# mLSTM decode state update: one fused VectorE operation per sample in place of two GpSimd operations per four samples

## The chip, the cores and the metric

The kernel runs on one core of a Trainium2 chip. The metric is the device time of one execution in microseconds (us), the median over repeated runs. A profile of a single execution stands beside it. Its engines are called PE (TensorE), ACT (ScalarE), DVE (VectorE), POOL (GpSimd) and SP (SyncE, which here only issues DMAs). Each engine works through its own instructions strictly in order, and an instruction that waits holds up everything behind it on that engine.

## What is computed

One inference step of a two-layer decoder for 256 prompt tokens and 8 single-token samples, which share the weights (264 columns in all). Layer 0 mixes tokens with a convolution, layer 1 with an mLSTM; each has a convolutional feed-forward block and an embedding gate behind it. The change concerns the mLSTM state of the 8 samples, where each has a matrix memory of 128 x 256 for each of 8 heads:

```python
def step(carry, inp):                       # for a sample: one token, so one step
    c, n, m = carry
    ...
    num = (s @ v) + (q @ c) * w_inter       # the OLD c is read for the output
    ...
    g_state = jnp.exp(inter[..., -1] - m_new)
    g_tok = jnp.exp(bh[..., -1:] - bh + lih - m_new[..., None])
    c_new = g_state[..., None, None] * c + jnp.einsum('bhs,bshk,bshv->bhkv', g_tok, kc, vc)
```

For a sample the last line is: new state = a number of the head and sample times the old state, plus an outer product of k and v (v already weighted).

## The kernel before, in words

All big products go through `wblock`: a weight block of 4 x 128 rows by 512 columns is loaded by one DMA (`raw`, three buffers), ACT makes its rounded upper part (`whi`, line 234), DVE the rest (`wlo`, line 235), and PE multiplies three times for each 128 x 128 piece (lines 250, 252, 253, and 259 for a first piece). Five buffers of two such row groups let ACT and DVE run ahead of PE. The issuing order on each engine is chosen by the framework's list scheduler, which simulates the time; `high_priority` moves an instruction ahead in it, `after` fixes an order.

In layer 1, `mlstm` works on pairs of heads. `project(pr)` computes q, k, v of a pair; `heads(pr)` runs the steps of four generators in turn: `prompt` of two heads and `sample` of two heads. PE meanwhile goes on with the next products (`opened` for the gate, the next `project`). `norm` normalises the outputs of a pair: its two matmuls (`hm`, line 825, and `hq`, line 833) are put between the matmuls of a later block (`normed`), each behind a given one, and they need sums from DVE.

The change is in `Head.sample`. Per head there are two groups of four samples (`b4` = 0, 1). `Ct` (state) and `kb` (rows q and k) are pieces of the big tile `X`, which is parked in DRAM meanwhile; they show in the profile as `X`. The two heads of a pair use the same two `Ct` places, so the load of the second head's group waits for the store of the first head's group. For each group:

- SP issues the load of `Ct` (line 795) and of `kb` (796).
- DVE multiplies `Ct` with q (two operations of 128 x 512, in the profile `spare<-X`) and sums over k (`tensor_reduce`, line 801): these become the output of the samples, via four tiny 128 x 16 operations per head (`spare<-qc`, `spare<-spare,sv`, or `H<-...` for the last pair).
- ACT replaces `kb` by the outer product, eight operations of 128 x 128 (line 805).
- POOL multiplies the four states by their numbers (`X<-X,spare`) and adds `kb` (`X<-X`), each 128 x 1024.
- SP issues the store (line 808).

There are 8 heads x 2 groups = 16 groups. The helper `tt` records its operations at line 138, `stt` (scalar_tensor_tensor, DVE only) at line 141. Besides, POOL has at the end of `mlstm` four small operations for the feed-forward's past rows (`sf`, `fo`).

Of the kernel before, what the change touches and what calls it, by code (L numbers as in the profile page):

```python
# [15 lines left out]
ALU = mybir.AluOpType  # L16
AX = mybir.AxisListType

P = 128
# [89 lines left out]
def _body(ctx, tc, nc, I, O):  # L109
    PSUM = bass.MemoryType.PSUM  # L110
    v, s, g, pe, dma = nc.vector, nc.scalar, nc.gpsimd, nc.tensor, nc.sync
# [19 lines left out]
    def misc(name):  # L131
        return psM.tile([P, 512], F32, name=name, tag="mi")
# [4 lines left out]
    def tt(o, a, b, op, e=v):  # L137
        return e.tensor_tensor(o, a, b, op)  # L138

    def stt(o, a, sc, b, op0, op1):  # L140
        return v.scalar_tensor_tensor(o, a, sc, b, op0, op1)  # L141

    def after(ins, first):

        tc.add_manual_dep(ins.ins, first.ins.name, mybir.DependencyInfo(
            mybir.DependencyClass.NoSync, mybir.DependencyReason.DATA), reason="order")
# [473 lines left out]
    def mlstm(xin):  # L620
# [82 lines left out]
        class Head:  # L703
# [65 lines left out]
            def sample(self):  # L769
                h, vh, H, den, bwi, bwf = self.h, self.v, self.H, self.den, self.bwi, self.bwf  # L770
                qs, ks = self.q[:, SEQ:], self.k[:, SEQ:]
                qq = smp.tile([P, 2, NB], F32, name="qq", bufs=2)
                tt(qq[:, 0], qs, ks, ALU.mult)
                tt(qq[:, 1], qs, sn[:, h], ALU.mult)
                nf = smp.tile([P, NB], F32, name="nf", bufs=2)
                tt(nf, sn[:, h], bwf, ALU.mult)
                tt(NS[:, h], ks, bwi, ALU.mult)
                tt(NS[:, h], NS[:, h], nf, ALU.add)
                vw = smp.tile([P, 2, NB], F32, name="vw", bufs=2)
                tt(vw, vh[:, :, SEQ:], bwi.unsqueeze(1).to_broadcast([P, 2, NB]), ALU.mult)  # L780
                psq = misc("sq")
                pe.matmul(psq[:, 0:2 * NB], ones, qq.rearrange("p a b -> p (a b)"), start=True, stop=True)
                ss = smp.tile([P, 2, NB], F32, name="ss", bufs=2)
                tt(ss, psq[:, 0:2 * NB].rearrange("p (a b) -> p a b", a=2),
                   self.bc[:, 648:664].rearrange("p (a b) -> p a b", a=2), ALU.mult)
                tt(den[:, SEQ:], ss[:, 0], ss[:, 1], ALU.add)
                stt(den[:, SEQ:], den[:, SEQ:], -1.0, den[:, SEQ:], ALU.mult, ALU.max)
                yield
                yield
                yield  # L790
                qc = smp.tile([P, NB, 2], F32, name="qc", bufs=2)
                for b4 in range(2):
                    Ct, kb = (XF[:, o + b4 * 1024:o + b4 * 1024 + 1024].rearrange("p (b x k) -> p b x k", b=4, x=2)
                              for o in (0, 2048))
                    dma.dma_start(Ct, I["cT"][h, :, 4 * b4:4 * b4 + 4])
                    dma.dma_start(kb, rows[h, 4 * b4:4 * b4 + 4].partition_broadcast(P))
                    for b2 in (0, 2):
                        qp = s1[:, 512 + 4 * T:1024 + 4 * T].rearrange("p (b x k) -> p b x k", b=2, x=2)
                        ins = tt(qp, Ct[:, b2:b2 + 2], kb[:, b2:b2 + 2, 0:1, :].to_broadcast([P, 2, 2, P]), ALU.mult)
                        after(ins, self.pt)  # L800
                        v.tensor_reduce(qc[:, 4 * b4 + b2:4 * b4 + b2 + 2], qp, AX.X, ALU.add)
                    for bi in range(4):
                        e = 4 * b4 + bi
                        for x in range(2):
                            act(kb[:, bi, x], kb[:, bi, 1], AF.Copy, scale=vw[:, x, e:e + 1])
                    tt(Ct, Ct, bwf[:, 4 * b4:4 * b4 + 4].unsqueeze(2).unsqueeze(3).to_broadcast([P, 4, 2, P]), ALU.mult, e=g)
                    tt(Ct, Ct, kb, ALU.add, e=g)
                    dma.dma_start(O["cT"][h, :, 4 * b4:4 * b4 + 4], Ct)
                    yield
                hs = H[:, :, SEQ:]  # L810
                tt(hs, qc.rearrange("p b x -> p x b"), bwf.unsqueeze(1).to_broadcast([P, 2, NB]), ALU.mult)
                sv = smp.tile([P, 2, NB], F32, name="sv", bufs=2)
                tt(sv, vh[:, :, SEQ:], ss[:, 0].unsqueeze(1).to_broadcast([P, 2, NB]), ALU.mult)
                tt(hs, hs, sv, ALU.add)
# [289 lines left out]
```

## Time and profile before

| what | us |
|---|---|
| median of 3 runs (2585.0 to 2591.87) | 2591.32 |
| the profiled execution, its own time | 2594.45 |
| its span | 2592.6 |
| PE busy | 2524.0 (97%) |
| DVE busy | 1680.9 (65%) |
| ACT busy | 1286.0 (50%) |
| POOL busy | 395.2 (15%) |

The shares are means over stages with different limits. The mLSTM stage with the sample updates lies at about 1300 to 1640 us of the span; the first of the 32 POOL operations starts at 1307.1, the last at 1614.1.

A view in order of time gives for each instruction the start and the duration in us, engine, line, operation, what is written and read, and in square brackets the idle time before it on its engine with the last releaser. Grouped views give busy time in us and the mean duration in ns.

### The profile page before, as it was taken

What the parts mean: (1) busy time and instruction counts of PE and PEld (TensorE: products, weight loads), DVE (VectorE), ACT (ScalarE), POOL (GpSimd) and SP (SyncE); (2) the same over time, 40 slices, a digit from 0 to 9 for tenths busy, and PEclk for the clock granted to TensorE, in tenths of its full rate; (3) what the DMA queues carried; (4) which work ended last, traced back from release to release, by engine and by line L of the source; (5) the groups of instructions that cost most, each with busy time, mean ns of one, the idle gap of its engine ahead of it and who ended that gap; (6) DMA issues with size and microseconds to landing.
All of it is one profiled execution on the core that took longest, in us unless ns stands there. A gap on an engine that the chain in (4) does not pass through costs nothing.

```text
span 2592.6 us, 47730 instructions
## 1 busy us (share of the span) xinstructions
PE 2524.0 (97%) x20130; PEld 2499.7 (96%) x20130; DVE 1680.9 (65%) x2318; ACT 1286.0 (50%) x1801; POOL 395.2 (15%) x352
## 2 busy tenths in 40 slices
PE   8898999999999999999989998999999999999999
PEld 8897999999999999999989998999999999999999
DVE  6999686555445555488678778685555445555595
ACT  5666555444334444356456666374444334444363
POOL 7898120000000000020031123020000000000020
PEclk9999999999999999999999999999999999999999
DMA  7546445555555556545666776645555555556554
GB/s 251 172 132 203 164 149 194 177 187 182 182 180 179 179 179 207 180 167 195 208 225 217 238 242 214 220 148 196 188 181 179 179 179 179 180 180 204 178 175 138
DMA packets 266697, 486.57 MB, mean 188 GB/s; under 512 B 12362, under 2 KB 68426, under 8 KB 265938
## 3 DMA queue, kind: packets, MB, share of 16 engines
q1 hardware_dynamic: 266482, 483.52, 56.9%
q8 instruction: 157, 2.57, 0.4%
q14 instruction: 58, 0.48, 0.1%
HBM read 465.77 MB, written 19.68 MB: 187 GB/s over the span
## 4 chain that ended last, share of the span: by engine, by line
PE 83%; DVE 6%; DMA 3%; POOL 3%; issue 2%; ACT 2%; SPq 0%; POOLq 0%; DVEq 0%; ACTq 0%
PE acc L253 27%; PE acc L250 27%; PE acc L252 23%; PE acc L259 3%; DVE wlo L235 1%; POOL cscr L138 1%; DVE Y L141 1%; DMA X<-in_cT 1%; DMA out_cT<-X 1%; DVE spare L138 1%; DVE Y L138 1%; POOL wlo L235 1%; PE acc L452 1%; ACT whi L234 1%; POOL u L504 0%
## 5 line engine op out<-in xcount | busy, mean ns | idle before, releaser
L235 DVE TENSOR_TENSOR wlo<-raw,whi 128x1024 fp32r<-128x1024 f32 (+1 forms) x770 | 977.3, 1274 | 815.0 <-ACT whi L234 767.7
L234 ACT CAST whi<-raw 128x1024 fp32r<-128x1024 f32 x812 | 846.0, 1045 | 1019.9 <-PE acc L252 972.6
L253 PE MATMUL acc<-XH,wlo 128*128 128x264 f32 x4264 | 1192.0, 286 | 14.4 <-POOL wlo L235 7.9
L250 PE MATMUL acc<-XH,whi 128*128 128x264 f32 x4264 | 1193.7, 286 | 5.9 <-ACT cscr L546 4.9
L252 PE MATMUL acc<-XL,whi 128*128 128x264 f32 x3696 | 1049.7, 285 | 0.0
L253 PEld LDWEIGHTS acc<-XH,wlo 128*128 128x128 f32 x4264 | 803.7, 189 | 17.4 <-POOL wlo L235 9.6
L250 PEld LDWEIGHTS acc<-XH,whi 128*128 128x128 f32 x4264 | 801.7, 189 | 8.3 <-ACT cscr L546 5.3
L252 PEld LDWEIGHTS acc<-XL,whi 128*128 128x128 f32 x3696 | 701.4, 190 | 0.1
L235 POOL TENSOR_TENSOR wlo<-raw,whi 128x1024 fp32r<-128x1024 f32 (+1 forms) x42 | 97.4, 2324 | 1670.3 <-DVE X L138 1506.1
L253 PE MATMUL acc<-ha,wlo 128*128 128x264 f32 x1024 | 290.2, 285 | 0.0
L250 PE MATMUL acc<-ha,whi 128*128 128x264 f32 x1024 | 288.6, 285 | 0.0
L252 PE MATMUL acc<-ha,whi 128*128 128x264 f32 x960 | 272.0, 284 | 0.0
L250 PE MATMUL acc<-xo,whi 128*128 128x264 f32 x768 | 225.4, 295 | 8.0 <-ACT so L894 6.0
L253 PE MATMUL acc<-xo,wlo 128*128 128x264 f32 x768 | 223.8, 293 | 0.0
L252 PE MATMUL acc<-xo,whi 128*128 128x264 f32 x720 | 211.3, 294 | 0.0
L253 PEld LDWEIGHTS acc<-ha,wlo 128*128 128x128 f32 x1024 | 193.2, 189 | 0.0
L250 PEld LDWEIGHTS acc<-ha,whi 128*128 128x128 f32 x1024 | 192.0, 189 | 0.1
L252 PEld LDWEIGHTS acc<-ha,whi 128*128 128x128 f32 x960 | 181.4, 189 | 0.1
L250 PEld LDWEIGHTS acc<-xo,whi 128*128 128x128 f32 x768 | 148.9, 194 | 9.5 <-ACT so L894 6.4
L253 PEld LDWEIGHTS acc<-xo,wlo 128*128 128x128 f32 x768 | 149.1, 194 | 0.8
L252 PEld LDWEIGHTS acc<-xo,whi 128*128 128x128 f32 x720 | 139.6, 194 | 0.7
L138 POOL TENSOR_TENSOR cscr<-cscr 128x254 f32<-128x254 f32 (+10 forms) x140 | 124.7, 918 | 11.5 <-ACT cscr L564 10.3
(284 smaller groups left out, 2580.0 us busy)
## 6 DMA issues: line engine op xcount, KB each, us to landing
raw<-in_ff_w_gate SPq DMA_DIRECT2D x88, 1024.0 KB, 5.1
raw<-in_ff_w_up SPq DMA_DIRECT2D x88, 1024.0 KB, 5.1
raw<-in_ff_w_down SPq DMA_DIRECT2D x88, 1024.0 KB, 5.0
raw<-in_pl_w_gate SPq DMA_DIRECT2D x32, 1024.0 KB, 5.0
raw<-in_ml_w_in SPq DMA_DIRECT2D x32, 1024.0 KB, 6.2
raw<-in_cv_w_in SPq DMA_DIRECT2D x48, 512.0 KB, 5.0
raw<-in_cv_w_out SPq DMA_DIRECT2D x16, 1024.0 KB, 5.0
raw<-in_ml_w_in SPq DMA_DIRECT2D x32, 512.0 KB, 5.3
```

Of the source, the lines that this page charges most:

```text
L138: return e.tensor_tensor(o, a, b, op)
L141: return v.scalar_tensor_tensor(o, a, sc, b, op0, op1)
L234: whi = s.copy(hi[:, :, :width], r)
L235: wlo = e.tensor_tensor(lo[:, :, :width], r, f32(hi[:, :, :width]), ALU.subtract)
L250: pe.matmul(acc[j], wh, xh, start=kc == 0, stop=False)
L252: pe.matmul(acc[j], wh, xl, start=False, stop=False)
L253: wlast[0] = pe.matmul(acc[j], wl, xh, start=False, stop=not lag and kc == nk - 1)
L259: pe.matmul(acc[j], whs[j], xl, start=False, stop=lag > 0 and k0_ == nk - 1)
L452: po(pe.matmul(acc, w[:, k, j * P:(j + 1) * P], pt[:, k], start=k == 0, stop=k == 1))
```

## The change

For each group the two POOL operations are replaced by four `scalar_tensor_tensor` operations on DVE, one per sample: Ct = Ct x number + kb, over 128 x 256. The number is read per partition from `bwf`.

```diff
                     for bi in range(4):
                         e = 4 * b4 + bi
                         for x in range(2):
                             act(kb[:, bi, x], kb[:, bi, 1], AF.Copy, scale=vw[:, x, e:e + 1])
-                    tt(Ct, Ct, bwf[:, 4 * b4:4 * b4 + 4].unsqueeze(2).unsqueeze(3).to_broadcast([P, 4, 2, P]), ALU.mult, e=g)
-                    tt(Ct, Ct, kb, ALU.add, e=g)
+                    for bi in range(4):
+                        e = 4 * b4 + bi
+                        stt(Ct[:, bi], Ct[:, bi], bwf[:, e:e + 1], kb[:, bi], ALU.mult, ALU.add)
                     dma.dma_start(O["cT"][h, :, 4 * b4:4 * b4 + 4], Ct)
                     yield
```

## Rows read from the trace of the kernel before

**Rows 1.** Per stretch: length, PE, PEld, DVE, ACT, POOL busy, clock, DMA share, GB/s

```profile
0.00:1300.00 1300.00, 1263.89 (x9995) 1247.89 (x9995) 857.69 (x1236) 655.63 (x898) 274.83 (x278) 0.99 0.57 184
1300.00:1640.00 340.00, 316.09 (x2447) 311.27 (x2448) 267.61 (x383) 204.90 (x414) 81.04 (x36) 0.96 0.68 230
1640.00:2592.00 952.00, 943.98 (x7691) 940.56 (x7689) 555.63 (x699) 425.48 (x489) 39.36 (x38) 1.00 0.55 178
```

**Rows 2.** PE in order of time, 1300 to 1640 us: its idle times over 1 us

```profile
1301.49 0.39 PE L250 MATMUL acc<-xo,whi 128*128 128x264 f32 x1 [1.97 <-ACT vv L876]
...
1338.53 0.46 PE L250 MATMUL acc<-xo,whi 128*128 128x264 f32 x1 [4.42 <-ACT so L894]
1361.31 0.71 PE L833 MATMUL hq<-hq,onesD 128*128 128x264 f32 x2 [2.02 <-DVE hq L138]
1426.09 0.39 PE L250 MATMUL acc<-xo,whi 128*128 128x264 f32 x1 [1.60 <-ACT so L894]
1451.56 1.25 PE L833 MATMUL hq<-hq,onesD 128*128 128x264 f32 x2 [4.17 <-DVE hq L138]
1516.90 1.25 PE L825 MATMUL hm<-hm,onesD 128*128 128x264 f32 x2 [2.64 <-DVE hm L138]
1595.41 1.25 PE L825 MATMUL hm<-hm,onesD 128*128 128x264 f32 x2 [4.80 <-DVE hm L138]
1617.77 0.49 PE L833 MATMUL hq<-hq,onesD 128*128 128x264 f32 x1 [1.80 <-DVE hq L138]
```

**Rows 3.** POOL, groups by form, 1300 to 1640 us: busy us, mean ns | idle

```profile
L138 POOL TENSOR_TENSOR X<-X 128x1024 f32<-128x1024 f32 x16 | 44.0, 2753 | 9.4 <-POOL X L138 4.4 <-ACT X L805 2.3 <-issue 1.5
L138 POOL TENSOR_TENSOR X<-X,spare 128x1024 f32<-128x1024 f32 x16 | 33.1, 2070 | 289.3 <-DVE spare L138 133.0 <-ACT vt L740 72.3 <-ACT X L805 69.6
```

**Rows 4.** DVE, groups by form, 1300 to 1640 us

```profile
L235 DVE TENSOR_TENSOR wlo<-raw,whi 128x1024 fp32r<-128x1024 f32 x90 | 126.4, 1405 | 37.3 <-ACT whi L234 34.1 <-PE hm L825 1.8 <-PE acc L252 1.1
L138 DVE TENSOR_TENSOR spare<-X 128x512 f32<-128x512 f32 x32 | 27.2, 850 | 14.7 <-DMA X<-in_cT 14.3
L801 DVE TENSOR_REDUCE qc<-spare 128x4 f32<-128x512 f32 x32 | 21.8, 681 | 0.6
...
L138 DVE TENSOR_TENSOR qw<-qk,spare 128x128 f32<-128x128 f32 x8 | 8.9, 1106 | 0.0
L138 DVE TENSOR_TENSOR spare<-qc,spare 128x16 f32<-128x16 f32 x6 | 8.6, 1432 | 0.1
...
L141 DVE SCALAR_TENSOR_TENSOR spare<-spare,par,so 128x264 f32<-128x264 f32 x12 | 5.3, 489 | 2.6 <-ACT so L894 2.5
...
L141 DVE SCALAR_TENSOR_TENSOR Pd<-qw,cn,spare 128x128 f32<-128x128 f32 x8 | 2.8, 346 | 0.7 <-ACT cn L746 0.6
...
L138 DVE TENSOR_TENSOR vw<-vv,spare 128x16 f32<-128x16 f32 x8 | 1.4, 171 | 0.0
```

**Rows 5.** DVE, groups by form, 1750 to 2592 us

```profile
L235 DVE TENSOR_TENSOR wlo<-raw,whi 128x1024 fp32r<-128x1024 f32 x278 | 341.0, 1231 | 349.8 <-ACT whi L234 329.0 <-PE acc L252 20.7
```

**Rows 6.** DVE in order of time, ahead of the idle time at 1361.31

```profile
1356.25 2.42 DVE L235 TENSOR_TENSOR wlo<-raw,whi 128x1024 fp32r<-128x1024 f32 x1
1358.59 2.33 DVE L138 TENSOR_TENSOR spare<-qc,spare 128x16 f32<-128x16 f32 x1
```

**Rows 7.** A stretch of 10 us, columns as in the first group

```profile
1360.00:1370.00 10.00, 8.69 (x57) 8.62 (x58) 8.91 (x20) 6.51 (x12) 0.88 (x1) 0.83 0.93 327
```

**Rows 8.** The DMA queue's waits, 1300 to 1640 us: total us, times, longest

```profile
SPq L795 <- DMA out_cT<-X: 27.9, 10, 6.3
SPq L808 <- POOL X L138: 23.9, 6, 6.6
```

**Rows 9.** DVE and ACT in order of time, one group: last reduce, last of eight scales

```profile
1398.51 0.69 DVE L801 TENSOR_REDUCE qc<-spare 128x4 f32<-128x512 f32 x1
1400.45 0.71 ACT L805 ACTIVATE X<-X,vw 128x128 f32<-128x128 f32 x2
```

**Rows 10.** POOL in order of time: the first operation of the feed-forward's past rows

```profile
1588.72 1.49 POOL L939 COPY fo<-sf 128x352 f32<-128x352 f32 x1
```

## The prediction

> **What bounds the kernel now.** I read the table of stretches first. PE is busy for nearly all of the first and last stretch, but in the mLSTM stage (1300 to 1640 us) only 316.1 of 340 us, and its granted clock is 0.96 there against 1.00 behind it [rows 1]. So PE sets the time, and this stage can give back at most what PE loses in it: 340 - 316.1 = 23.9 us idle, and by the clock about 0.04 x 340 = 13.6 us. Nothing outside the stage is touched; the stretches before and after count as they are.
>
> PE in order of time then shows that the idle time is a few stalls: 1.97, 4.42, 2.02, 1.60, 4.17, 2.64, 4.80 and 1.80 us, together 23.4 [rows 2]. The first comes before any of the POOL operations can hold anything and stays. Of the other seven (21.5 us), five wait for `hm` or `hq`, sums that DVE delivers late, and two for `so`, which ACT delivers late behind things that wait for DVE. So in this stage the engine ahead of PE is DVE: 267.6 of 340 us busy [rows 1], in order, and late at the ends of the head pairs. The question is whether the change takes time from DVE or gives it.
>
> **What goes.** POOL loses 16 + 16 operations, 33.1 + 44.0 = 77.1 us [rows 3]. Nobody waits for POOL as such except the stores. But DVE pays while POOL runs: the weight split `wlo`, the same form, takes 1405 ns on the mean here [rows 4] and 1231 ns in the later stages [rows 5]; a 128 x 16 product takes 1432 ns where another of that size takes 171; the 128 x 128 product `qw` takes 1106 ns where the fused operation of that size takes 346; the 128 x 512 products take 850 ns, the reduces of the same size 681 [rows 4]. A tiny operation at 2.33 us [rows 6], about as long as a POOL operation (2.07 and 2.75 us on the mean) [rows 3], says that DVE is held until POOL is done. The held time by those four pairs of rows: 90 x 0.174 = 15.7, 6 x 1.261 = 7.6, 8 x 0.760 = 6.1, 32 x 0.169 = 5.4: 34.8 us, a lower bound since smaller forms are left out. That is 2.2 us for each of the 16 groups. All of it goes with POOL's operations.
>
> The Trainium skill ("SBUF — State Buffer", "Who interferes with whom") says that a VectorE instruction with two SBUF inputs and a GpSimd instruction that reads SBUF exclude each other for a whole instruction, and that a reduce never contends. The trace agrees as to the reduces, 32 at a mean of 681 ns [rows 4]. By that rule the new operations, which have two SBUF inputs, can themselves be held by what POOL keeps; that is the fourth rival below.
>
> **What comes.** 64 fused operations of 128 x 256 on DVE. The trace has none of this very shape; the nearest with all inputs in SBUF and a per-partition number are 489 ns at 264 columns and 346 ns at 128 [rows 4]. The end at 346 would make 22.1 us, the end at 489 31.3 us. I take 0.40 us, an estimate: 256 lies near 264, and successive DVE operations overlap by some 0.08 us (2.42 us after 1356.25 is 1358.67, and the next starts at 1358.59 [rows 6]), so 489 ns cost the queue about 0.40. That is 25.6 us, 1.6 for a group. DVE's balance is -34.8 + 25.6 = -9 us for the stage, -0.6 per group at least.
>
> **Where it lies.** Mean values say too little, since only the groups just ahead of a stall matter. Ahead of the stall at 1361.31 the held time is 2.42 - 1.23 = 1.2 for `wlo` and 2.33 - 0.17 = 2.2 for the tiny product, 3.4 us [rows 4 to 6]; four fused operations add 1.6: 1.8 us net of a stall of 2.02. I take 0.6 to 1.8 us per group. Three of the seven stalls come behind one group (1361, 1451, 1617): 3 x 0.6 to 3 x 1.8, so 1.8 to 5.4. The other four (1338, 1426, 1516, 1595) come at the end of a pair's dense part, behind two groups: 4 x 1.2 to 2 x 3.6 + 1.6 + 2.64 (two are no longer than that), so 4.8 to 11.4. Sum: 6.6 to 16.8 us. I take 13, in the upper half, since in the one stall worked out the upper value holds, and since the held time is a lower bound.
>
> **The clock.** After a stall the granted clock is lower for a while, 0.83 in the ten us with the stall of 2.02 [rows 7], where the level falls from 2.4 to 1.2 GHz for part of the time. It goes with the stalls: 13 of 23.9 us of idle time are 54%, and 54% of 13.6 is 7 us (3 to 10 for the ends).
>
> **The queues.** SP waits 23.9 us for POOL before stores, and 27.9 us for stores before it issues the loads of the next `Ct` [rows 8]; DVE in turn waits 14.3 us for those loads [rows 4]. A group's POOL part is 2.07 + 2.75 = 4.8 us; four fused operations are 1.6, so the store goes some 3 us sooner, and the next group's load and sums with it. I count this at nothing: where it helps, it eats into the same stalls. The weight loads queue behind these waits on SP; no stall of PE names them [rows 2], and they come sooner, if anything.
>
> **The added wait.** The fused operations need ACT's scales, and now stand in DVE's own queue. What is queued behind them is `wlo`, the tiny products and `hm`, `hq`, for which PE waits. Bounds: nothing, if the list scheduler puts other DVE work ahead of them, and 1401.16 - 1399.20 = 2.0 us per group, the time from the end of the last reduce to the end of the last scale in one group [rows 9], so 32 us if nothing fills it anywhere. I take a tenth for PE: 2 us, because the first samples of a group can be done while the last are scaled, and `wlo` is there to fill in.
>
> **Sum.** 13 + 7 - 2 = 18 us less. Against the profiled execution: 2594.45 - 18 = 2576.5 us. That execution lies 3.1 us above the median of the runs (2591.32), so the forecast for the median is 2573.3, a gain of 0.7%. Its own range: 2563 (16.8 + 10 - 0, 27 us off, and a little) to 2583.
>
> **The rivals.**
> First, a larger gain: the stalls but the first vanish, as DVE's held time is more than counted and the stores go 3 us sooner. 21.5 + 0.9 x 13.6 = 33.7 us at most; at three quarters of it 25, so 2566, and lower at the very end. For it speaks the DVE wait on `in_cT`; against it that 4.17 and 4.80 us are longer than any net relief I can work out.
>
> Second, no change: the stalls are set by DMA. The sums at a pair's end come from the second head's `Ct`, whose load waits for a store and then takes its own time; DVE's idle 14.3 us [rows 4] are for that. If `hm` and `hq` come no sooner, DVE's relief falls into its idle time. Then only the two stalls behind `so` shrink: 3 us at most, 2588. Against it: in rows 6 DVE is busy up to the late sum.
>
> Third, slower: the scheduler puts the four fused operations directly behind the reduces, and DVE stands for ACT, in every group. 2.0 + 1.6 = 3.6 us per group against 2.2 held: +1.4 for a group; the eleven groups ahead of the seven stalls make 15 us at worst, some 12 with part of it covered: 2603. It decides from the point where the wait per group is above 2.2 - 1.6 = 0.6 us, which one group shows as possible [rows 9]. Against it: ACT is busy only 204.9 of 340 us [rows 1], and the scheduler sees the wait.
>
> Fourth, the change does not clear POOL: the feed-forward's operations stay, the first 1.49 us long at 1588.72 [rows 10], ahead of the longest stall (4.80). If DVE's products are held by these four (6 us at most, if all were as long), that stall stays: 3.6 us less of the sum, and 2 of clock: 2579. It lies within the forecast's range.
>
> **How the numbers follow.** A measurement of this kernel can tell about 0.3% (7.8 us) from no change. Forecast, fourth rival included: 0.52. Larger gain 0.13. No change 0.22. Slower 0.13, of which a fifth would stay within 0.3%. So faster 0.65, same 0.25, slower 0.10. The range leaves out about 2 in 10: from 2562, most of the larger gain inside, to 2595, the no-change case inside and slower outside.
>
> **What would show it.** Right: `wlo` at about 1230 ns in the stage, no 128 x 16 operation over 0.5 us but near the feed-forward's POOL operations; 64 fused operations at 0.43 to 0.49 us; PE idle in the stage at about 11 us, clock at 0.98; store waits of SP shorter. Wrong: DVE idle before the fused operations with ACT's scales as the releaser (third rival), or DVE idle for `in_cT` as long as before with the stalls in place (second). It would also be wrong if the scheduler, with other costs to plan with, laid out the stage anew and put `hm` and `hq` earlier among the matmuls, so that as much is waited for as before.

## The result, and the profile after

| | before | after |
|---|---|---|
| median, us | 2591.75 (6 runs) | 2573.43 (6 runs, 2571.09 to 2581.83) |
| ratio | | 0.9937, 95% interval 0.9919 to 0.9954 |
| profiled execution, span, us | 2592.6 | 2573.7 |

The change makes the kernel faster by 0.63% (0.46 to 0.81%), 18.3 us by the medians; 18.0 were forecast. The median of before is taken over three more runs than ahead of the prediction.

The stretches of after, columns as in [rows 1] (length, PE, PEld, DVE, ACT, POOL busy, granted clock, DMA share, GB/s); the last one ends sooner, since the span does:

```profile
0.00:1300.00 1300.00, 1263.63 (x9995) 1247.46 (x9995) 857.64 (x1237) 655.36 (x898) 274.19 (x278) 0.99 0.57 184
1300.00:1640.00 340.00, 326.25 (x2606) 320.57 (x2607) 255.24 (x460) 212.30 (x422) 4.66 (x4) 0.99 0.73 243
1640.00:2570.00 930.00, 924.57 (x7531) 921.12 (x7529) 543.12 (x686) 417.11 (x481) 39.37 (x38) 1.00 0.56 177
```

The first stretch is as before. In the mLSTM stage PE idles 340 - 326.25 = 13.75 us in place of 23.9, and its clock is 0.99 in place of 0.96 [rows 1]. DVE has 64 operations more and is still less busy, though more of the work now falls into the same 340 us (2606 of PE's matmuls in place of 2447).

DVE by form in the same stage (busy us, mean ns | idle before); the answer to [rows 4]:

```profile
L235 DVE TENSOR_TENSOR wlo<-raw,whi 128x1024 fp32r<-128x1024 f32 x98 | 119.5, 1223 | 30.9 <-ACT whi L234 24.5 <-PE acc L252 3.2 <-PE acc L253 2.8
L141 DVE SCALAR_TENSOR_TENSOR X<-X,spare 128x256 f32<-128x256 f32 x64 | 29.1, 489 | 0.0
L138 DVE TENSOR_TENSOR spare<-X 128x512 f32<-128x512 f32 x32 | 22.6, 705 | 16.4 <-DMA X<-in_cT 16.3
L801 DVE TENSOR_REDUCE qc<-spare 128x4 f32<-128x512 f32 x32 | 21.7, 679 | 0.2
...
L138 DVE TENSOR_TENSOR qw<-qk,spare 128x128 f32<-128x128 f32 x8 | 2.3, 285 | 0.0
...
L138 DVE TENSOR_TENSOR spare<-qc,spare 128x16 f32<-128x16 f32 x6 | 1.0, 168 | 0.0
```

Every form that was slow beside POOL is at its undisturbed time: `wlo` 1223 ns (1405 before), `qw` 285 (1106), the tiny product 168 (1432); the reduces are as they were (679, before 681). The 64 fused operations take 489 ns each, and DVE stood idle ahead of none of them (0.0).

The page's totals over the whole span, after:

```profile
PE 2514.4 (98%) x20130; PEld 2489.2 (97%) x20130; DVE 1656.2 (64%) x2382; ACT 1284.8 (50%) x1801; POOL 318.2 (12%) x320
```

PE does the same 20130 matmuls in 2514.4 us of busy time where it took 2524.0, and idles 2573.7 - 2514.4 = 59.3 us of the span where it idled 68.6: of the 18.9 us by which the span is shorter, 9.3 are idle time and 9.6 busy time, at a granted clock of 0.994 over the span in place of 0.989. DVE falls from 1680.9 to 1656.2 us, by 24.7, although it took on the fused operations. Two of these in a row, from the view in order of time:

```profile
1351.37 0.87 DVE L141 SCALAR_TENSOR_TENSOR X<-X,spare 128x256 f32<-128x256 f32 x2
1352.16 0.68 DVE L138 TENSOR_TENSOR spare<-X 128x512 f32<-128x512 f32 x1
```

The next one starts 0.79 us after the first of the two, so each costs DVE's queue 0.395 us, 64 of them 25.3. What POOL's operations had held of DVE is then 24.7 + 25.3 = 50 us, an estimate from one such spacing.

PE in order of time in the stage, idle times over 1 us, after; the answer to [rows 2]:

```profile
1301.44 0.39 PE L250 MATMUL acc<-xo,whi 128*128 128x264 f32 x1 [1.53 <-ACT vv L877]
1322.76 0.71 PE L755 MATMUL num<-spare,vt 128*128 128x128 f32 x4 [1.75 <-ACT spare L761]
1357.07 0.71 PE L834 MATMUL hq<-hq,onesD 128*128 128x264 f32 x2 [2.54 <-DVE hq L138]
...
1600.58 0.51 PE L253 MATMUL acc<-XH,wlo 128*128 128x264 f32 x2 [1.55 <-DVE wlo L235]
1603.58 0.51 PE L253 MATMUL acc<-XH,wlo 128*128 128x264 f32 x2 [1.27 <-DVE wlo L235]
1608.64 1.13 PE L834 MATMUL hq<-hq,onesD 128*128 128x264 f32 x2 [2.94 <-DVE hq L138]
```

Between 1358 and 1600 us, no stall over 1 us is left; there had been four behind the one at 1361.31. The long ones (4.42, 4.17, 4.80) are gone as such. But the stall at the first pair's `hq` is longer (2.54, before 2.02), and at the end of the last pair the waiting has mostly moved: 1.55 + 1.27 + 2.94 = 5.8 us from 1600.58 on, where 4.80 + 1.80 = 6.6 stood. What went, went mainly between these two places.

SP's waits in the stage, after; the answer to [rows 8]:

```profile
SPq L795 <- DMA out_cT<-X: 37.0, 12, 6.9
...
SPq L809 <- DVE spare L138: 14.4, 4, 4.1
SPq L809 <- DVE X L141: 14.2, 7, 4.6
```

SP waits no less than before, ahead of the stores (14.4 + 14.2, before 23.9) as ahead of the loads (37.0, before 27.9).

### The profile page after: what moved, and what is told of

Its sections match the earlier page's. It is cut to its first block, busy times and chain, and to the rows that moved or that the text cites. A ratio compares the mean times of both kernels' runs of the same rounds, so it can differ in the third digit from the quotient of the medians.

```text
span 2573.7 us, 47727 instructions
## 1 busy us (share of the span) xinstructions
PE 2514.4 (98%) x20130; PEld 2489.2 (97%) x20130; DVE 1656.2 (64%) x2382; ACT 1284.8 (50%) x1801; POOL 318.2 (12%) x320
## 4 chain that ended last, share of the span: by engine, by line
PE 86%; DVE 5%; DMA 3%; POOL 3%; issue 2%; ACT 1%; SPq 0%; POOLq 0%; DVEq 0%; ACTq 0%
PE acc L253 27%; PE acc L250 27%; PE acc L252 24%; PE acc L259 3%; POOL cscr L138 1%; DMA out_cT<-X 1%; DVE wlo L235 1%; POOL wlo L235 1%; DVE Y L138 1%; PE acc L452 1%; DVE Y L141 1%; DMA X<-in_cT 1%; DMA spare<-scr 1%; PE acc L226 1%; POOL u L504 0%
## 5 line engine op out<-in xcount | busy, mean ns | idle before, releaser
L235 DVE TENSOR_TENSOR wlo<-raw,whi 128x1024 fp32r<-128x1024 f32 (+1 forms) x770 | 960.0, 1252 | 801.7 <-ACT whi L234 751.0
L250 PE MATMUL acc<-xo,whi 128*128 128x264 f32 x768 | 221.4, 289 | 2.2 <-ACT vv L877 1.5
L252 PE MATMUL acc<-xo,whi 128*128 128x264 f32 x720 | 207.7, 289 | 0.0
L250 PEld LDWEIGHTS acc<-xo,whi 128*128 128x128 f32 x768 | 144.6, 188 | 3.3 <-ACT vv L877 1.7
L252 PEld LDWEIGHTS acc<-xo,whi 128*128 128x128 f32 x720 | 135.9, 189 | 0.6
L138 POOL TENSOR_TENSOR cscr<-cscr 128x254 f32<-128x254 f32 (+10 forms) x140 | 123.8, 909 | 11.6 <-ACT cscr L564 10.4
```

Of the source, the lines that this page charges most:

```text
L235: wlo = e.tensor_tensor(lo[:, :, :width], r, f32(hi[:, :, :width]), ALU.subtract)
L250: pe.matmul(acc[j], wh, xh, start=kc == 0, stop=False)
L252: pe.matmul(acc[j], wh, xl, start=False, stop=False)
```

## The experiments

Three theories stood against each other. **Held:** the gain is DVE time that POOL's reading operations had taken. **Chain:** it comes from stores that wait for POOL no more, and so from sooner loads of `Ct`. **Layout:** the scheduler laid out the stage anew, and the new order happens to be better.

**POOL reads again, for nothing.** Both of the first two runs keep the changed kernel and its order of instructions on PE, DVE, ACT and SP, instruction for instruction; only POOL has work besides. In the other runs the scheduler made another order.

```diff
+        held = smp.tile([P, 896], mybir.dt.bfloat16, name="held")
...
+                    hv, pv8 = (q[:, :896].rearrange("p (b x k) -> p b x k", b=4, x=2) for q in (held, par))
+                    for src in range(2): tt(hv, pv8, qc[:, 4 * b4:4 * b4 + 4].unsqueeze(3).to_broadcast([P, 4, 2, 112]), ALU.mult, e=g)
```

> The changed kernel, and for each of the 16 groups POOL also does two products of 128 x 896 that read two SBUF operands and write to a scratch tile that nobody reads; they start when the group's sums are there, about when the POOL operations of the kernel before did. The order of the instructions on DVE, ACT and SP is that of the changed kernel, and no store waits for POOL. Held theory (the gain is DVE time that POOL's operations had held): DVE is held again by 25 to 40 us, with the fused operations still there, so the gain is lost and more: 2590 to 2612 us, tiny 128 x 16 operations at over 1 us on the mean. Chain theory (the gain comes from sooner stores and loads of Ct) and layout theory (it comes from the new order of the instructions): 2573 us, as the changed kernel.

Measured: 2601.91 us, ratio to before 1.0049 (1.0031 to 1.0066): the gain is gone, and 11.6 us more. Stage and forms of this run, views as above, with POOL's own form:

```profile
1300.00:1640.00 340.00, 309.85 (x2392) 303.80 (x2393) 281.81 (x439) 202.03 (x411) 69.06 (x36) 0.96 0.67 228
```

```profile
L235 DVE TENSOR_TENSOR wlo<-raw,whi 128x1024 fp32r<-128x1024 f32 x88 | 111.0, 1264 | 19.8 <-ACT whi L234 14.2 <-PE acc L253 2.8 <-DMA raw<-in_ml_w_in 1.3
L141 DVE SCALAR_TENSOR_TENSOR X<-X,spare 128x256 f32<-128x256 f32 x64 | 49.1, 800 | 0.0
...
L801 DVE TENSOR_REDUCE qc<-spare 128x4 f32<-128x512 f32 x32 | 21.7, 678 | 0.3
...
L138 DVE TENSOR_TENSOR spare<-qc,spare 128x16 f32<-128x16 f32 x6 | 5.5, 913 | 0.0
```

```profile
L138 POOL TENSOR_TENSOR held<-par,qc 128x896 bf16<-128x896 f32 x32 | 64.0, 2000 | 321.4 <-DVE qc L801 320.3
```

Nobody uses what POOL makes here, no store waits for it, and the order is that of the changed kernel. Still PE idles 30.2 us in the stage and its clock is back at 0.96. Here it is mostly the fused operations themselves that are held: 800 ns in place of 489. `wlo` is held little (1264), the tiny product less than expected (913 ns, over 1 us had been), the reduce, which has one input, not at all (678). One fused operation beside POOL:

```profile
1335.71 1.90 DVE L141 SCALAR_TENSOR_TENSOR X<-X,spare 128x256 f32<-128x256 f32 x1
```

```profile
1333.76 3.57 POOL L138 TENSOR_TENSOR held<-par,qc 128x896 bf16<-128x896 f32 x2 [6.08 <-DVE qc L801]
```

POOL's two operations end at 1337.33, the held one at 1337.61.

**POOL as busy, but only writing.**

```diff
+                    g.tensor_copy(held[:, 0:8], qc[:, 4 * b4:4 * b4 + 4].rearrange("p b x -> p (b x)"))
+                    for src in range(5): g.memset(held, 0.0)
```

> The same as the run with POOL reads, but POOL only writes: five memsets of the scratch tile for each group (and one copy of 8 columns that starts them). Held theory with reads as the cause: 2573 us give or take 5, wlo at about 1230 ns. If any busy POOL slows DVE: as with the reads, 2590 us or more.

Measured: 2571.74 us, ratio 0.9931 (0.9916 to 0.9946), the changed kernel's time.

```profile
L235 DVE TENSOR_TENSOR wlo<-raw,whi 128x1024 fp32r<-128x1024 f32 x99 | 120.6, 1220 | 35.4 <-ACT whi L234 29.0 <-PE acc L252 3.1 <-PE acc L253 2.8
L141 DVE SCALAR_TENSOR_TENSOR X<-X,spare 128x256 f32<-128x256 f32 x64 | 29.1, 489 | 0.0
```

```profile
L808 POOL MEMSET held<- 128x896 bf16 x80 | 67.6, 845 | 4.5
```

67.6 us of memsets hold nothing that shows: `wlo` and the fused operations are as fast as without. (The 16 copies that start the memsets read 8 columns each.) The two runs differ in what POOL does alone, and by 2601.91 - 2571.74 = 30.2 us. So it is the reads that hold DVE, not a busy POOL, and the hold alone, in one and the same order of instructions, is worth more than the whole gain. Layout can't make that difference. It could still have a part in the 18.3 us between before and after, whose orders differ; but the four runs below that do the update without POOL's reads or leave it out (no update, late stores, fused operations twice, ACT multiplies) have orders of their own, and all are faster than before. This is what the Trainium skill says ("SBUF — State Buffer", "Who interferes with whom"): a VectorE instruction with two SBUF inputs contends with a GpSimd instruction that reads SBUF, not with one that only writes it.

**No update at all.**

```diff
-                    for bi in range(4):
-                        e = 4 * b4 + bi
-                        stt(Ct[:, bi], Ct[:, bi], bwf[:, e:e + 1], kb[:, bi], ALU.mult, ALU.add)
```

> The changed kernel without the fused operations: the state update is left out, Ct is stored as it was loaded. DVE is free of POOL's holds and of 64 x 0.4 to 0.49 us of its own. Held theory, with PE paying for DVE time about as in the change (18.9 us of span for 24.7 us of DVE): the stage's idle PE time goes from 13.7 us to 4 to 8, so 2562 to 2569 us. Chain theory: the stores go 1.6 us sooner per group, a third of what the change brought: 2566 to 2570 us. If what is left of the stalls is not DVE's doing: 2572 us.

Measured: 2566.29 us, ratio 0.9910 (0.9895 to 0.9925). Without hold and without fused operations the kernel gains 7.1 us over the changed one (2573.43), 5.5 over the run in which POOL only writes (2571.74): that is what the fused operations cost, if held theory is right. The order is another one here, so the number is good to some us only. The time lies in the range of held theory and in that of chain theory, so this run does not part the two; the next one does.

**The latency without the hold.**

```diff
-                    for bi in range(4):
-                        e = 4 * b4 + bi
-                        stt(Ct[:, bi], Ct[:, bi], bwf[:, e:e + 1], kb[:, bi], ALU.mult, ALU.add)
+                    for src in range(5):
+                        g.memset(Ct, 0.0)
```

> The changed kernel with the state update left out, and in its place five POOL memsets of the group's Ct (128 x 1024, about 0.95 us each), so that the store waits for POOL about as long as in the kernel before, while POOL reads nothing and DVE has no fused operations. Held theory: as the run without update, 2562 to 2570 us. Chain theory: the late stores alone bring back the loss: 2585 us or more.

Measured: 2563.72 us, ratio 0.9902 (0.9885 to 0.9918). Five memsets of 956 ns stand ahead of each store, as long as POOL's 2.07 + 2.75 us in the kernel before [rows 3]:

```profile
L807 POOL MEMSET X<- 128x1024 f32 x80 | 76.2, 956 | 269.4 <-DVE spare L138 196.4 <-ACT X L805 69.5
```

```profile
SPq L795 <- DMA out_cT<-X: 34.0, 13, 5.3
...
SPq L808 <- POOL X L807: 21.1, 12, 4.6
```

SP waits for POOL and for the stores about as in [rows 8], POOL is as busy as before (395.3 us, before 395.2), and the median is the lowest of all. So the chain through the stores is worth nothing that shows: chain theory falls. Nor did SP wait less in the changed kernel itself. Read against the kernel before, this run takes away the hold and keeps the latency: 2590.35 (before, beside this run) - 2563.72 = 26.6 us is the hold's price there, but for what the other order of instructions does.

**Half of the change, twice.** With `b4 == 0` on POOL and `b4 == 1` on DVE, and the other way round:

```diff
+                    if b4 == 0:
+                        tt(Ct, Ct, bwf[:, 4 * b4:4 * b4 + 4].unsqueeze(2).unsqueeze(3).to_broadcast([P, 4, 2, P]), ALU.mult, e=g)
+                        tt(Ct, Ct, kb, ALU.add, e=g)
-                    for bi in range(4):
+                    for bi in range(4 if b4 == 1 else 0):
```

> Half of the change: the first group of each head (b4 = 0) is done by POOL as before, the second by fused DVE operations. Held theory: the stalls stand at the ends of the pairs, behind second groups, so most of the gain stays: 2572 to 2580 us. If only DVE's total time counted: half of the gain, 2582 us.

> The other half: the first group of each head by fused DVE operations, the second (b4 = 1) by POOL as before. Held theory: the holds are again just ahead of the sums that PE waits for, so most of the gain is lost: 2584 to 2592 us. If only DVE's total time counted: 2582 us.

Measured: 2578.64 us (ratio 0.9952, 0.9937 to 0.9967) with POOL early and 2578.89 us (0.9951, 0.9936 to 0.9965) with POOL late. The second was expected to lose most of the gain and did not. At neither place did the hold of one half cost more than at the other, against what the prediction and the held theory as first put had it. But DVE's total alone does not give the numbers either: for that, half of the gain was expected (2582 us), and beside their own before (2592.67) the halves gain 14.0 and 13.8 us, three quarters of the 18.3. DVE's busy time fell by 1680.9 - 1665.7 = 15.2 and 1680.9 - 1669.7 = 11.2 us of the change's 24.7. The intervals of the halves and of the whole change overlap, so their distance is known to some us only. In both, the forms near POOL are slow again, others in each: `qw` with POOL early, the tiny product with POOL late (early first, then late):

```profile
L138 DVE TENSOR_TENSOR qw<-qk,spare 128x128 f32<-128x128 f32 x8 | 8.9, 1108 | 0.0
L138 DVE TENSOR_TENSOR spare<-spare,sv 128x16 f32<-128x16 f32 x6 | 1.0, 169 | 0.0
L138 DVE TENSOR_TENSOR spare<-qc,spare 128x16 f32<-128x16 f32 x6 | 1.0, 168 | 0.0
```

```profile
L138 DVE TENSOR_TENSOR spare<-qc,spare 128x16 f32<-128x16 f32 x6 | 6.9, 1150 | 0.1
L138 DVE TENSOR_TENSOR spare<-spare,sv 128x16 f32<-128x16 f32 x6 | 3.2, 527 | 0.1
L138 DVE TENSOR_TENSOR qw<-qk,spare 128x128 f32<-128x128 f32 x8 | 2.3, 285 | 0.0
```

**The fused operations twice.**

```diff
+                    for bi in range(4):
+                        e = 4 * b4 + bi
+                        stt(qp[:, bi % 2], Ct[:, bi], bwf[:, e:e + 1], kb[:, bi], ALU.mult, ALU.add)
```

> The changed kernel with every fused operation done a second time into a scratch place: 64 more operations on DVE, 25 to 31 us more of DVE time in the stage, stores no later. Prices DVE time for PE. Held theory with DVE as the engine ahead of PE: 2582 to 2598 us. If DVE has room in this stage (chain or layout theory): 2573 to 2577 us.

Measured: 2581.67 us, ratio 0.9960 (0.9947 to 0.9973), 8.2 us above the changed kernel, 0.3 below the range that was expected. Taken by the gains, each over the before measured beside it, it is 18.3 - (2592.67 - 2581.67) = 7.3. 64 more operations (about 25 us of DVE's queue) cost PE a third of that. It agrees with the 7.1 us of the run without update.

**A version in which ACT multiplies.**

```diff
-                        stt(Ct[:, bi], Ct[:, bi], bwf[:, e:e + 1], kb[:, bi], ALU.mult, ALU.add)
+                        act(Ct[:, bi], Ct[:, bi], AF.Copy, scale=bwf[:, e:e + 1])
+                    tt(Ct, Ct, kb, ALU.add)
```

> A version that might beat both: ACT multiplies the four states by their numbers (64 operations of 128 x 256), DVE only adds kb (16 operations of 128 x 1024, about 1.23 us each, 20 us in place of 29). Held theory with the price that the doubled run gives (about 10 us for 29 us of DVE time): 9 us less of DVE give 2 to 3 us, 2570 us, if ACT, 19 to 25 us busier, is not late for that. If ACT is as near to the bound as DVE: 2573 to 2580 us.

> The changed kernel itself beside the run in which ACT scales, on the same chip, so that the two can be compared directly: 2573 us.

Measured: 2577.26 us (ratio 0.9947, 0.9934 to 0.9959) against 2575.55 us (0.9953, 0.9939 to 0.9966) for the changed kernel beside it. No difference that can be told. DVE's part is smaller as planned, but ACT's is 29.1 us, and a stall of 5.30 us for ACT's `so` stands in the profile of this run:

```profile
L808 ACT ACTIVATE X<-X,spare 128x256 f32<-128x256 f32 x64 | 29.1, 503 | 0.0
L138 DVE TENSOR_TENSOR X<-X 128x1024 f32<-128x1024 f32 x16 | 19.8, 1238 | 3.0 <-ACT X L805 2.9
```

```profile
1560.36 0.59 PE L250 MATMUL acc<-xo,whi 128*128 128x264 f32 x1 [5.30 <-ACT so L896]
```

## Why the prediction was right, point by point

**What bounds the kernel.** Right. All of the gain lies in the mLSTM stage, in PE's stalls and its clock, and DVE is the engine ahead of PE there: the hold moves the time by 30.2 us in one order of instructions.

**What goes.** The mechanism was right, the size too small: 34.8 us of held time were counted from four forms, called a lower bound; the trace of after makes it 50, and the run with the late stores, which has neither hold nor fused operations, 1680.9 - 1632.6 = 48.3. Among what the four forms left out are the other tiny products, such as `spare<-spare,sv`, 882 ns before and 168 after.

**What comes.** 0.40 us per fused operation was estimated, 0.395 was measured. Their price for PE is some 6 to 10 us of 25, by the run that doubles them and the two that leave them out.

**Where it lies.** This step got its sum nearly right for a partly wrong reason. 13 us of stalls were to go; 23.9 - 13.75 = 10.2 went. But the stall worked out in full, 2.02 us for `hq` at 1361.31, was to shrink to 0.2, and is 2.54 us in the trace of after. DVE waits there for the load of `Ct` first, and had done so before as well; [rows 6] begin behind that wait, so that DVE seemed busy all along. Before, then after:

```profile
1352.46 0.69 DVE L138 TENSOR_TENSOR spare<-X 128x512 f32<-128x512 f32 x1 [2.87 <-DMA X<-in_cT]
```

```profile
1349.03 0.69 DVE L138 TENSOR_TENSOR spare<-X 128x512 f32<-128x512 f32 x1 [2.96 <-DMA X<-in_cT]
```

From there to the sum for `hq` DVE took 8.0 us (to 1357.01), before 8.8, but PE, which had stalled less earlier, came to its place sooner as well. So for this stall the second rival was right. Half of its sign shows in the whole stage: DVE idles 16.3 us for `in_cT`, before 14.3 [rows 4], though half of the stall time is gone. The relief was counted group by group, just ahead of each stall; the two halves of the change show that it is not the groups just ahead of the stalls alone that count, since relief in either group of each head brought the same. The longest stalls fell whole, 4.42 and 4.17 us, where the working had them lose at most 3.6 and 1.8. That relief carries over from group to group is argued from this, not shown step by step; and the price of a microsecond of DVE was not the same in every run, as the last section has it.

**The clock.** 7 us expected; 0.99 - 0.96 of 340 us is 10, with two digits in either clock. The totals of the span say the same: 9.6 us less of PE's busy time for the same matmuls, and 9.3 less of idle time.

**The queues.** Counted at nothing, and right: the run with the late stores is as fast as any. But SP's store waits, which were to be shorter, are not: the store now waits for DVE as it had waited for POOL.

**The added wait.** 2 us were taken off for it. It did not come: DVE's idle time ahead of the fused operations is 0.0. The third rival needed it in every group. The scheduler put the four operations apart: in the rows of after two stand behind a reduce, with the next product behind them.

**The fourth rival.** The feed-forward's POOL operations now run at 1568 us, and the stall of 4.80 us is gone as such. They do hold what DVE runs beside them:

```profile
1569.11 0.72 DVE L141 SCALAR_TENSOR_TENSOR X<-X,spare 128x256 f32<-128x256 f32 x1
1569.75 1.29 DVE L138 TENSOR_TENSOR spare<-X 128x512 f32<-128x512 f32 x1
1570.96 1.02 DVE L141 SCALAR_TENSOR_TENSOR X<-X,spare 128x256 f32<-128x256 f32 x1
```

With the `wlo` behind them (1.56 us) that is some 1.7 us over the usual times, where 6 at most had been allowed for.

The errors of the terms (stalls 3 too many, clock 3 too few, wait 2 too many, rounding) cancel in part; the closeness of the sum is luck within its range, the sign and the mechanism are not. A second account from the runs: the hold out of the kernel before gives 26.6 us, the fused operations take back 7 to 8 (the doubled run), which leaves 18 to 19. Measured were 18.3; both prices come with orders of their own.

## What to carry to other kernels

Work on GpSimd that reads SBUF is not free beside a busy VectorE: here 77 us of it took some 50 us from VectorE, about twice what the same work costs when VectorE does it itself. Look for it by comparing the mean time of one form with and without GpSimd beside it, above all at tiny operations that take 2 us. And where an engine's lateness reaches the bounding one through many small stalls, count its time over the stage as well; taking single stalls apart came near the sum here, but not by the stalls that really went.

## What had not been expected of the hardware

The hold is not tied to one kind of VectorE operation: the fused operation with a per-partition number went from 489 to 800 ns on the mean beside reading GpSimd operations. Writing alone, 67.6 us of GpSimd memsets in one run and 76.2 in another, left VectorE's forms at their undisturbed times. And PE's time answered to VectorE's in unlike parts. VectorE's busy time on the pages of five runs, in this order: POOL reads, POOL writes, the fused operations twice, no update, the late stores without the hold:

```profile
PE 2522.7 (97%) x20130; PEld 2497.3 (96%) x20130; DVE 1700.3 (65%) x2382; ACT 1285.8 (49%) x1801; POOL 383.6 (15%) x352
```

```profile
PE 2516.2 (98%) x20130; PEld 2492.3 (97%) x20130; DVE 1657.4 (64%) x2382; ACT 1285.6 (50%) x1801; POOL 398.3 (15%) x416
```

```profile
PE 2518.8 (98%) x20130; PEld 2493.2 (97%) x20130; DVE 1682.0 (65%) x2446; ACT 1286.1 (50%) x1801; POOL 321.9 (12%) x320
```

```profile
PE 2513.0 (98%) x20130; PEld 2490.0 (97%) x20130; DVE 1636.0 (64%) x2318; ACT 1287.1 (50%) x1803; POOL 319.1 (12%) x320
```

```profile
PE 2511.5 (98%) x20130; PEld 2487.9 (97%) x20130; DVE 1632.6 (64%) x2318; ACT 1285.3 (50%) x1801; POOL 395.3 (15%) x400
```

Putting the hold back added 1700.3 - 1657.4 = 42.9 us to VectorE and 30.2 to the time, 0.70 for each; taking it out of the kernel before, with the stores still late, took 48.3 and 26.6, 0.55 for each; the fused operations done twice added 1682.0 - 1656.2 = 25.8 and 8.2, 0.32 for each; leaving them out took 1656.2 - 1636.0 = 20.2 and 7.1, 0.35 for each. So a microsecond of hold cost about twice a microsecond of work; only the first of the four pairs has one order of instructions. The scheduler laid out another order for the work, but not for the hold (the order was the same with it and without), which besides comes in lumps of some 2 us; which of these makes the difference the runs don't tell.
